# A two-layer hybrid trunk: layer 0's FFN and layer 1 run in context and latent halves, RWKV and GDN with one joint inverse and joint links

## The chip, the cores and the metric

The kernel runs on one core of a Trainium2 chip. TensorE (PE) does the matmuls into PSUM, VectorE (DVE), ScalarE (ACT) and GpSimd (POOL) the element work, SyncE (SP) issues the transfers between DRAM and SBUF. The metric is the device time of one execution in microseconds; of several runs the median is given.

## The reference

The input is 256 latent tokens `x` and 256 context tokens `ctx`, each of 1024 channels. Two layers follow one another. In each, four mixers read the same normed input, their outputs are gated and summed, and a SwiGLU FFN follows. The recurrent mixers start on the context, in both directions, and the latent half starts from the context's final state. `with_ctx` is true in layer 0 alone: layer 1 gives no context output, and of its context half only states, keys and values are used.

```python
def _rwkv7_mixer(pa, ca, ..., with_ctx):
    lat, ctx = _rwkv7_inputs(pa, ...), _rwkv7_inputs(ca, ...)
    for d in range(2):
        s_c, yc = _rwkv7_scan(ctx, d, s0, d == 1)
        _, yl = _rwkv7_scan(lat, d, s_c, d == 1)
    ...
def _mixer_block(h, hc, w_in, ...):
    p, pc = h @ w_in, hc @ w_in
    ...                     # RWKV-7, gated DeltaNet (GDN), GLA, window attention
    out = _merge((ya, yb, yg, yd), gl, gate_b, w_branch, w_out)
def _merge(ys, gate_pre, gate_b, w_branch, w_out):
    for i, y in enumerate(ys):
        g = sigmoid(gate_pre[..., i * D_MODEL:(i + 1) * D_MODEL] + gate_b[i])
        acc = acc + g * (y @ w_branch[i])
    return acc @ w_out
def _swiglu(h, w1, w2):
    gt, up = jnp.split(h @ w1, 2, axis=-1)
    return (jax.nn.silu(gt) * up) @ w2
```

## The kernel before

Channels lie on the partitions, tokens on the free axis, 512 columns: tiles 0 and 1 are the context, 2 and 3 the latents. A float32 product is made of three rounded ones. A weight block of 128x1024 (512 KB) is fetched as `raw`, rounded by ScalarE to `whi` (line 180), and VectorE subtracts to get `wlo` (line 183); with the input split into `hh` and `hl` a block gives 24 matmuls (16 with `whi`, 8 with `wlo`, line 193). Products go to three PSUM banks for this work: two of kind "f", one of kind "m".

`layer` (line 1383) does a whole layer. It norms the input, and makes the columns of `w_in` it needs: `dense_f` on all 512 columns for keys, values and states, in layer 1 on the 256 latent ones for queries and gates. `rwkv` and `gdn` bring the chunks of 64 tokens to triangular systems, and each inverts all of its own in `tri_inverse` (60 small VectorE operations on tiles `lx` and `lt`, a trip through DRAM tiles `dl`, `dx`, then products `v`). Then each has a chain of eight links, both directions in lockstep, whose small products (`psc`, 64x64) wait for one another through VectorE. High priority puts the inverse's steps and the links first. The 32 gate blocks (`w_gate`) have a low priority and fill what the chains leave; in GDN's chain `early` fills with the first 16 units of the merge (a unit is six matmuls with `yp`, a product with the gate `g`, and an addition into `acc1`). The other units and the last branch follow, then `residual` with `w_out`, and the FFN: 44 blocks of `ffn_w1`, whose hidden tiles are split at once into `uh` and `ul`, and 22 blocks of `ffn_w2` in `residual`. Beside layer 0's FFN `ada_f` (line 1245) makes layer 1's conditioning on VectorE: 160 products `gr` (or `gj`) of 128x512, line 1258.

The order of the instructions on each engine is set when the program is built, by a scheduler that takes them in the program's order and priority, with its own costs, as PSUM and SBUF buffers come free.

## Time and profile before

| | us |
|---|---|
| median of 3 runs | 1799.29 |
| lowest, highest run | 1786.75, 1800.61 |
| profiled execution | 1792.01 |
| its span | 1790.2 |
| TensorE busy | 1662.3 |
| VectorE busy | 1100.1 |
| ScalarE busy | 830.2 |
| GpSimd busy | 144.3 |
| mean granted TensorE clock | 0.958 |

Busy shares are means over stretches that differ. Layer 0's mixer ends at about 625 us, its merge and `w_out` at 717.5, its FFN at 1094; layer 1's mixer with merge and `w_out` ends at 1594.8, then comes its FFN. The clock is the share of full speed that was granted to TensorE.

### The profile page before, as it was taken

How to read it: one execution, taken by the hardware profiler on the slowest of the kernel's cores; microseconds unless marked ns; L12 is line 12 of the kernel's file. 1: busy time of each engine (PE TensorE's matmuls, PEld its weight loads, DVE VectorE, ACT ScalarE, POOL GpSimd, SP SyncE). 2: the span in 40 equal slices, each digit the busy share in tenths (PEclk: the TensorE clock that was granted, in tenths of full speed). 3: DMA queues.
4: the chain of work that ended last, by engine and by line, in shares of the span. 5: the costliest groups of instructions: out<-in, count | busy, mean ns of one | idle time of the engine just before them, and what ended most of it. 6: DMA issues, size and time to landing. Idle time of an engine off the chain costs nothing. (4 is left out here: it accounts for less than half of the span.)

```text
span 1790.2 us, 31565 instructions
## 1 busy us (share of the span) xinstructions
PE 1662.3 (93%) x12480; PEld 1328.0 (74%) x12480; DVE 1100.1 (61%) x2243; ACT 830.2 (46%) x1440; POOL 144.3 (8%) x255
## 2 busy tenths in 40 slices
PE   6999999998998979999999999998899869889998
PEld 3777775666786657888877888777777757779986
DVE  3466643447936765899675226666677665766654
ACT  3565442355534224544333226763556441366653
POOL 0000111000002250000000000002021002400000
PEclk8999999998999989999999999999999877989999
DMA  8322554442552363566775223334533461445553
GB/s 336 115 98 89 157 149 165 154 146 71 146 148 71 100 197 106 174 223 216 238 249 160 94 95 106 113 121 137 160 113 98 113 191 61 133 158 185 188 200 118
DMA packets 149684, 263.71 MB, mean 147 GB/s; under 512 B 62224, under 2 KB 77088, under 8 KB 149408
## 3 DMA queue, kind: packets, MB, share of 16 engines
q1 hardware_dynamic: 149536, 261.69, 45.9%
q8 instruction: 98, 1.61, 0.4%
q14 instruction: 50, 0.41, 0.1%
HBM read 236.12 MB, written 25.53 MB: 146 GB/s over the span
## 5 line engine op out<-in xcount | busy, mean ns | idle before, releaser
L193 PE MATMUL pd<-hh,whi 128*128 128x512 f32 (+1 forms) x1648 | 549.0, 352 | 17.9 <-ACT g L171 5.0
L193 PE MATMUL pd<-hl,whi 128*128 128x512 f32 (+1 forms) x1648 | 546.1, 349 | 0.2 <-DVE hl L183 0.2
L183 DVE TENSOR_TENSOR wlo<-raw,whi 128x1024 fp32r<-128x1024 f32 x280 | 347.1, 1242 | 266.4 <-ACT whi L180 112.9
L180 ACT ACTIVATE whi<-raw 128x1024 fp32r<-128x1024 f32 x280 | 295.9, 1057 | 423.9 <-PE pd L193 245.4
L193 PEld LDWEIGHTS pd<-hh,whi 128*128 128x128 f32 x1648 | 317.3, 193 | 72.0 <-issue 9.6
L193 PEld LDWEIGHTS pd<-hl,whi 128*128 128x128 f32 x1648 | 316.6, 193 | 44.3 <-issue 6.1
L193 PE MATMUL pd<-hh,wlo 128*128 128x512 f32 (+1 forms) x1648 | 340.0, 346 | 5.2 <-DVE wlo L183 5.2
L193 PEld LDWEIGHTS pd<-hh,wlo 128*128 128x128 f32 x1648 | 264.3, 190 | 47.5 <-DVE wlo L183 5.6
L193 PE MATMUL t<-whi,ul 128*128 128x512 f32 x264 | 104.4, 395 | 0.0
L193 PE MATMUL t<-whi,uh 128*128 128x512 f32 x264 | 104.3, 395 | 0.0
L1258 DVE SCALAR_TENSOR_TENSOR gr<-gr,crow 128x512 f32<-128x512 f32 x112 | 75.5, 688 | 27.5 <-DMA gr<-in_ada_t_dram 26.6
L193 PE MATMUL t<-wlo,uh 128*128 128x512 f32 x264 | 75.2, 395 | 0.0
L193 PE MATMUL pd<-yp,whi 128*128 128x512 f32 (+1 forms) x192 | 57.9, 410 | 15.9 <-DVE g L183 13.0
L171 ACT ACTIVATE g<-g 128x512 f32<-128x512 f32 (+1 forms) x128 | 66.5, 522 | 2.9
L183 DVE TENSOR_TENSOR th<-th,pd 128x512 f32<-128x512 f32 (+1 forms) x88 | 48.6, 552 | 26.6 <-PE pd L193 24.6
L183 POOL TENSOR_TENSOR acc<-acc,g 128x512 f32<-128x512 f32 (+1 forms) x48 | 56.4, 1191 | 72.2 <-DVE g L183 72.0
L180 ACT ACTIVATE uh<-th 128x512 fp32r<-128x512 f32 (+1 forms) x44 | 23.1, 526 | 78.5 <-DVE th L183 78.2
L193 PEld LDWEIGHTS t<-whi,uh 128*128 128x128 f32 x264 | 49.8, 188 | 11.5 <-DVE yr L183 0.2
L193 PEld LDWEIGHTS t<-wlo,uh 128*128 128x128 f32 x264 | 49.7, 188 | 11.5
L193 PEld LDWEIGHTS t<-whi,ul 128*128 128x128 f32 x264 | 49.8, 188 | 11.4
L171 ACT ACTIVATE g<-pd,P 128x512 f32<-128x512 f32 (+1 forms) x64 | 37.0, 577 | 45.2 <-PE pd L193 33.0
L193 PEld LDWEIGHTS pd<-yp,whi 128*128 128x128 f32 x192 | 34.5, 217 | 27.0 <-DVE g L183 16.1
(366 smaller groups left out, 2272.7 us busy)
## 6 DMA issues: line engine op xcount, KB each, us to landing
raw<-in_ffn_w_dram SPq DMA_DIRECT2D x132, 512.0 KB, 3.3
raw<-in_w_gate_dram SPq DMA_DIRECT2D x64, 512.0 KB, 3.5
gr<-in_ada_t_dram SPq DMA_DIRECT2D x112, 256.0 KB, 3.3
raw<-in_w_in_dram SPq DMA_DIRECT2D x52, 512.0 KB, 3.2
raw<-in_ada_w_dram SPq DMA_DIRECT2D x40, 512.0 KB, 5.7
gd<-g SPq DMA_DIRECT2D x32, 256.0 KB, 2.5
raw<-in_w_branch_dram SPq DMA_DIRECT2D x16, 512.0 KB, 3.6
g<-gd SPq DMA_DIRECT2D x32, 256.0 KB, 3.5
```

Of the source, the lines that this page charges most:

```text
L171: return self.nc.scalar.activation(out=out, in_=in_, func=func, bias=bias, scale=scale, **kw)
L180: return self.nc.scalar.activation(out=out, in_=in_, func=ACTF.Copy, scale=scale)
L183: return (eng or self.nc.vector).tensor_tensor(out=out, in0=a, in1=b, op=op)
L193: self.last = self.nc.tensor.matmul(out, lhsT=lhsT, rhs=rhs, start=start, stop=stop, skip_group_check=skip)
L1258: nc.vector.scalar_tensor_tensor(out=raw if v == nv - 1 else junk, in0=raw, scalar=1.0, in1=self.cr[:, v, 512 * h:512 * h + 512], op0=ALU. ...
```

## The change

From layer 0's FFN on, context and latents are separate. `layer0` still runs the mixer on 512 columns. Its FFN runs on the context (tiles 0, 1) first: `ffn_in` with 44 blocks at 256 columns, then `residual` with `ffn_w2`. Then `context1` does layer 1's context half: norm, 13 blocks of `w_in` and the two of `lv` at 256 columns, the systems of RWKV and GDN (four chunks each, into one tile `TT`), one `tri_inverse` for both, and four links in which RWKV and GDN with both directions, four generators, go in lockstep. Final states, keys and values stay in `keep`. The FFN of the latents comes behind `context1` in the program, with both products in the two "f" banks. `layer1` then works on 256 columns: it has again one inverse and four joint links, the gates as low-priority fill, then RWKV's output, and behind it all 24 units of `early` and the last branch. So 44 + 22 + 15 weight blocks are loaded, rounded and subtracted once more. The hidden tiles are stored in float32 and split per `w2` block. The products of `ada_f` get their pool before `w_out` of layer 0, and 96 of 160 must be done before `context1`. In layer 0 GLA's loads are moved ahead of GDN's inverse (`step(4)`).

```diff
...
+    def splits(self, hid):
+
+        def at(pool):
+            def parts(k, m):
+                h, l = [pool.tile([128, m, hid.shape[2]], F32R, tag=t, name=self.nm(t), bufs=4) for t in ("hh", "hl")]
+                self.split(h, l, hid[:, k:k + m])
+                return h, l
+            return parts
+        return at
...
+    def ffn_in(self, l, hh, hl, hid, t, fu, step):
+
+        w1 = self.A["ffn_w1"][l]
+        n = hh.shape[2]
+        for j in range(22):
+            pg = self.dense_f(w1[0, j], hh, hl, "f")
+            th = t.tile([128, n], F32, tag="th", name=self.nm("th"))
+            self.sig(th, pg[:, 0:n])
+            self.tt(th, th, pg[:, 0:n])
+            pu = self.dense_f(w1[1, j], hh, hl, fu[j % len(fu)])
+            self.tt(hid[:, j], th, pu[:, 0:n])
+            step(j)
...
+            step(4)
+            for _ in inv:
+                step(2)
+            e2.close()
+            step(4)
...
+        ta = self.pool("ada", 2, es=ea, side="right")
+        xt = {**self.xload(0, xl, (2, 3)), **self.xload(0, xc, (0, 1))}
...
-                pg = first.pop(0) if first else self.dense_f(w1[0, j], hh, hl, qts, "f")
-                th = t.tile([128, 512], F32, tag="th", name=self.nm("th"))
-                self.sig(th[:, 0:n], pg[:, 0:n])
-                self.tt(th[:, 0:n], th[:, 0:n], pg[:, 0:n])
-                pu = first.pop(0) if first else self.dense_f(w1[1, j], hh, hl, qts, "m" if nxt else "mf"[j % 2])
-                self.tt(th[:, 0:n], th[:, 0:n], pu[:, 0:n])
-                self.split(uh[:, j], ul[:, j], th[:, 0:n])
-                for _ in range(2):
-                    next(more, None)
-        self.mark("ffn2%d" % l)
...
+        self.norm_h(nx, A2, B2, [((0, 1), hhc, hlc), ((2, 3), hhl, hll)])
+        self.cr = self.crow(ta)
+        ada = chain(self.ada_f(0, 5, 1, mod2[:, 24:32], self.adab, ta, 2), prep(1, ta))
+        self.ffn_in(0, hhc, hlc, hid, t, "mf", lambda j: next(ada))
+        e1.close()
+        self.mark("ffn20")
+        nx = self.residual(A["ffn_w2"][0], self.splits(hid), (0, 1), mod2[:, 24:32], R_NG3, xt, True, e2, lambda: 1 in self.par or next(ada))
+        ctx.close()
+        while 1 not in self.par:
+            next(ada)
+        hid = self.pool("hidl", 1, es=lat).tile([128, 22, 256], F32, name=self.nm("hid"))
+        self.use(1)
+        self.context1(nx, xc)
+        self.use(0)
+        self.mark("ffn1l0")
+        self.ffn_in(0, hhl, hll, hid, t, "f", lambda j: next(ada, None))
+        self.mark("ffn2l0")
+        nx = self.residual(A["ffn_w2"][0], self.splits(hid), (2, 3), mod2[:, 24:32], R_NG3, xt, True, e2, lambda: next(ada, None),
+                           lambda: self.psf("f"))
+        run(ada)
+        self.xsave = self.dram.tile([2, 128, 1024], F32, name=self.nm("xsave"))
+        for t in (2, 3):
...
+            ds = self.dense_set(1, hh, hl)
+            main = self.pool("mc", 1, es=es, side="right")
+            self.cp(K.misc[64:128, 0:256], ds.col("misc")[64:128, 0:256])
+            rw = self.rwkv_tiles(main, 4, False)
+            gd = self.gdn_tiles(main, 4, False)
+            TT = main.tile([128, 2, 2, 8, 64], F32, name=self.nm("TT"))
+            rw.TT, gd.TT = TT[:, :, :, 0:4], TT[:, :, :, 4:8]
+            rw.keep, gd.keep = K.Z, K.S
+            st = self.tri_begin()
+            self.mark("rwkv1c")
+            self.rwkv_prep(1, rw, ds.col, st, 0, K.FB)
+            self.mark("gdn1c")
+            self.gdn_prep(gd, ds.col, K.misc[96:128, 0:256], st, 4)
+            vf = main.tile([128, 256], F32, name=self.nm("vf"))
+            more = chain(ds.attn_kv(K.ak[:, 0:256], K.av[:, 0:2], vf), ds.gla_kv(K.lk, K.lv[:, 0:2]))
+            self.mark("tri1c")
+            with ExitStack() as e2:
+                for _ in self.tri_inverse(st, TT, self.pool("tri", 1, es=e2)):
+                    next(more, None)
+            run(more)
+            self.mark("chain1c")
+            ch = self.pool("ch", 2, es=es, side="right")
+            for s in range(4):
+                with HP():
+                    lockstep([f(o, s, d, ch, i + d) for d in range(2) for i, (f, o) in ((0, (self.rwkv_link, rw)), (2, (self.gdn_link, gd)))])
+        self.mark("end1c")
+
...
+        st = self.tri_begin()
+        self.mark("rwkv1")
+        self.rwkv_prep(1, rw, ds.col, st, 0, K.FB)
+        self.mark("gdn1")
+        self.gdn_prep(gd, ds.col, K.misc[96:128, 256:512], st, 4)
+        with self.tc.high_priority(offset=-2000):
...
+        self.rwkv_resume(rw, K.Z, ch)
+        gd.S = [K.S[:, 0], K.S[:, 1]]
+        sr, sd = set(), set()
+        for s in range(4):
+            with HP():
+                got = lockstep([f(o, s, d, ch, i + d) for d in range(2) for i, (f, o) in ((0, (self.rwkv_link, rw)), (2, (self.gdn_link, gd)))])
+            for d in range(2):
+                self.rwkv_emit(rw, d, got[2 * d], Yr, sr)
+                gl(3)
+                self.gdn_emit(gd, d, got[2 * d + 1], Yg, sd)
+                gl(3)
+        self.mark("out1")
+        with HP():
+            self.rwkv_out(1, rw, Yr, K.misc[0:64, 256:512], ydst(0))
+            for b in range(2):
+                self.rms_gate(Yg[:, b].rearrange("p n e -> p (n e)"), ydst(1)(b), sg[:, b], P[:, R_GDNG:R_GDNG + 1],
+                              TT[:, 0, b, 0:4].rearrange("p n i -> p (n i)"))
...
+        gl(500)
+        gl(1000)
+        mx.close()
+        mg = self.pool("m1", 2, es=ac)
+        acc1 = self.pool("ac1", 1, es=ac).tile([128, KD, n], F32, name=self.nm("acc1"))
+        run(self.early(1, [(i, lambda i=i: yparts[i]) for i in (3, 0, 1)], gdr, acc1, mg))
...
```

The first place is VectorE at the end of GDN's chain of layer 0. `U` belongs to the chain, `yp`, `acc` and `g` to the merge, `kf`, `qf`, `AS` to GLA. Before:

```order
L183 TENSOR_TENSOR acc_826_4978<-g_5096,pd_5098 128x512
L183 TENSOR_TENSOR kf_4940<-lqk_4542,EP_5039 128x512
L190 SCALAR_TENSOR_TENSOR qf_4939<-lqk_4542,EN_5040 128x512
L183 TENSOR_TENSOR acc_826_4978<-g_5135,pd_5137 128x512
L183 TENSOR_TENSOR AS_4943<-m_5064,c_lmask_4933 128x512
L183 TENSOR_TENSOR acc_826_4978<-g_5224,pd_5226 128x512
L183 TENSOR_TENSOR U_5335<-psc,TK_3881 128x128
L183 TENSOR_TENSOR AS_4943<-m_5071,c_lmask_4933 128x512
```

After (the last link, then what follows it):

```order
L185 TENSOR_TENSOR U_5994<-psc,gd_3862 128x128
L185 TENSOR_TENSOR Y_5050<-Y_5050,Y_5996 128x2x64
L185 TENSOR_TENSOR Y_5050<-Y_5050,Y_6017 128x2x64
L185 TENSOR_TENSOR wlo_5937<-raw_5934,whi_5936 128x1024
L185 TENSOR_TENSOR TT_3864<-Y_5050,TT_3864 128x512 x2
L192 SCALAR_TENSOR_TENSOR Y_5050<-TT_3864,P_105,sg_3773 128x512 x2
L185 TENSOR_TENSOR yp_5113<-y_5114,yp_5112 128x512
L185 TENSOR_TENSOR yp_5113<-y_5118,yp_5112 128x512
L185 TENSOR_TENSOR yp_5041<-Y_5050,yp_5040 128x512 x2
L185 TENSOR_TENSOR yp_5043<-lqk_4542,yp_5042 128x512
L185 TENSOR_TENSOR acc_842_5036<-g_5128,pd_5130 128x512
L185 TENSOR_TENSOR yp_5043<-lqk_4542,yp_5042 128x512
```

The products into `acc` of the first branch stood among the links (`U`, `Y`) and stand now behind the last of them.

The second place is VectorE where the inverse begins; `lx` and `lt` are its tiles, `th` and `hid` the latent FFN's. GDN's inverse in layer 1 before:

```order
L183 TENSOR_TENSOR lt_13370<-lt_13370,lx_13369 128x19x12
L183 TENSOR_TENSOR lx_13369<-lt_13370 128x234
L183 TENSOR_TENSOR lt_13370<-lt_13370,lx_13369 128x18x13
L183 TENSOR_TENSOR lx_13369<-lt_13370 128x238
L183 TENSOR_TENSOR lt_13370<-lt_13370,lx_13369 128x17x14
L183 TENSOR_TENSOR wlo_13702<-raw_13699,whi_13701 128x1024
L183 TENSOR_TENSOR lx_13369<-lt_13370 128x240
L183 TENSOR_TENSOR lt_13370<-lt_13370,lx_13369 128x16x15
```

The joint inverse of the context after, at its start:

```order
L185 TENSOR_TENSOR hid_9061<-th_11484,pd_11495 128x256
L185 TENSOR_TENSOR wlo_11566<-raw_11563,whi_11565 128x1024
L324 COPY lt_10083<-lx_10082 64x1024
L185 TENSOR_TENSOR th_11558<-th_11558,pd_11533 128x256
L185 TENSOR_TENSOR hid_9061<-th_11558,pd_11569 128x256
L185 TENSOR_TENSOR lx_10082<-lt_10083 128x30
L185 TENSOR_TENSOR lt_10083<-lt_10083,lx_10082 128x30
L185 TENSOR_TENSOR lx_10082<-lt_10083 128x58
L185 TENSOR_TENSOR lt_10083<-lt_10083,lx_10082 128x29x2
```

The last rows of the latent FFN (`th`, `hid`) before the steps stand there; the same inverse after, at its 28th step (128x17x14):

```order
L185 TENSOR_TENSOR lx_10082<-lt_10083 128x234
L185 TENSOR_TENSOR lt_10083<-lt_10083,lx_10082 128x18x13
L185 TENSOR_TENSOR lx_10082<-lt_10083 128x238
L185 TENSOR_TENSOR lt_10083<-lt_10083,lx_10082 128x17x14
L185 TENSOR_TENSOR wlo_10267<-raw_10264,whi_10266 128x1024
L185 TENSOR_TENSOR lx_10082<-lt_10083 128x240
L185 TENSOR_TENSOR wlo_11604<-raw_11601,whi_11603 128x1024
L185 TENSOR_TENSOR lt_10083<-lt_10083,lx_10082 128x16x15
L185 TENSOR_TENSOR lx_10082<-lt_10083 128x240
```

In both the steps stand in one piece up to 128x17x14; after, the pieces of the latent FFN (`hid`, `th`, the next `wlo`) stand ahead of and behind that piece.

The third place is TensorE in a chain. GDN's chain of layer 1 before (`psc` the links, `pd` merge units, `Y` the outputs):

```order
L193 MATMUL Y_14860<-qi_13211,S_14754 64x64 x3
L193 MATMUL psc<-S_14754,ke_13210 64x64 x4
L193 MATMUL psc<-S_14757,ke_13210 64x64 x4
L193 MATMUL Y_14860<-qi_13211,S_14754 64x64
L193 MATMUL pd_14872<-yp_14497,wlo_14781 128x256
L193 MATMUL Y_14881<-qi_13211,S_14757 64x64 x4
L193 MATMUL pd_14893<-yp_14497,whi_14780 128x256
L193 MATMUL pd_14893<-yp_14498,whi_14780 128x256
L193 MATMUL pd_14893<-yp_14497,whi_14780 128x256
```

The joint chain of the context after (`pd` a block of the latent FFN, `psc` the links):

```order
L195 MATMUL psc<-rw_9153,TT_9161 64x64 x3
L195 MATMUL psc<-gd_9155,TT_9161 64x64 x4
L195 MATMUL pd_11980<-hh_6675,whi_11976 128x256
L195 MATMUL pd_11980<-hh_6676,whi_11976 128x256
L195 MATMUL pd_11980<-hh_6675,whi_11976 128x256
L195 MATMUL pd_11980<-hh_6676,whi_11976 128x256
L195 MATMUL psc<-rw_9153,TT_9161 64x64
L195 MATMUL pd_11980<-hh_6675,whi_11976 128x256
L195 MATMUL pd_11980<-hh_6676,whi_11976 128x256
L195 MATMUL pd_11980<-hh_6675,whi_11976 128x256
L195 MATMUL pd_11980<-hh_6676,whi_11976 128x256
L195 MATMUL pd_11980<-hh_6675,wlo_11977 128x256 x4
```

The products of two branches now stand next to each other, and the cover between them is one FFN block in place of merge units.

## Rows read from the trace of the kernel before

**Rows 1.** The page, busy time of each engine (us, share of the span, instructions).

```profile
PE 1662.3 (93%) x12480; PEld 1328.0 (74%) x12480; DVE 1100.1 (61%) x2243; ACT 830.2 (46%) x1440; POOL 144.3 (8%) x255
```

**Rows 2.** Stretches: length, busy time of engines (x instructions), granted clock, DMA share, GB/s.

```profile
625.00:717.50 92.50, 77.72 (x311) 58.59 (x309) 55.05 (x72) 35.83 (x73) 27.76 (x19) 0.94 0.48 149
717.50:1094.00 376.50, 374.97 (x1680) 305.18 (x1681) 242.28 (x524) 142.75 (x214) 0.00 (x0) 0.99 0.53 175
1094.00:1594.80 500.80, 438.88 (x4399) 367.86 (x4397) 341.53 (x732) 260.00 (x503) 65.08 (x121) 0.91 0.43 129
1594.80:1790.20 195.40, 188.25 (x1321) 176.04 (x1321) 109.65 (x147) 105.88 (x168) 0.00 (x0) 0.98 0.50 167
```

**Rows 3.** Layer 1's mixer in eight stretches, columns as in group 2.

```profile
1094.00:1110.00 16.00, 13.38 (x86) 11.57 (x85) 14.17 (x26) 15.15 (x35) 0.24 (x3) 0.89 0.58 198
1110.00:1228.00 118.00, 109.42 (x992) 95.69 (x991) 77.38 (x121) 80.83 (x142) 6.96 (x15) 1.00 0.41 123
1228.00:1288.00 60.00, 51.44 (x457) 43.36 (x457) 39.31 (x93) 25.04 (x50) 4.91 (x7) 0.93 0.51 142
1288.00:1362.00 74.00, 71.27 (x849) 54.51 (x847) 54.44 (x127) 38.66 (x79) 16.60 (x48) 0.94 0.28 93
1362.00:1419.00 57.00, 50.36 (x539) 44.31 (x540) 39.84 (x71) 37.42 (x76) 5.85 (x7) 0.91 0.41 116
1419.00:1472.00 53.00, 37.94 (x360) 33.62 (x358) 36.65 (x86) 20.57 (x40) 0.16 (x1) 0.83 0.63 174
1472.00:1538.00 66.00, 60.23 (x891) 47.93 (x890) 40.13 (x142) 12.85 (x23) 13.43 (x22) 0.77 0.23 73
1538.00:1594.80 56.80, 44.84 (x238) 36.87 (x238) 39.61 (x72) 29.49 (x61) 16.93 (x18) 0.87 0.57 189
```

**Rows 4.** Matmuls of line 193 in two stretches of 50 us (512 columns, 256 columns).

```profile
1000.00:1050.00 50.00, 50.00 (x216) 40.44 (x215) 1.00 0.28 95
1600.00:1650.00 50.00, 50.00 (x424) 50.00 (x423) 1.00 0.55 180
```

**Rows 5.** A stretch of layer 0's FFN; layer 1's FFN: w1, w2.

```profile
750.00:850.00 100.00, 100.00 (x430) 80.44 (x429) 96.55 (x240) 40.81 (x54) 0.00 (x0) 1.00 0.66 218
...
1594.80:1722.40 127.60, 127.60 (x1061) 127.21 (x1062) 79.41 (x116) 82.06 (x137) 0.00 (x0) 0.99 0.53 177
1722.40:1783.00 60.60, 60.60 (x261) 48.83 (x260) 28.07 (x28) 22.64 (x28) 0.00 (x0) 1.00 0.44 150
```

**Rows 6.** Groups of instructions (busy, mean ns of one): page, then three stretches of VectorE.

```profile
L183 DVE TENSOR_TENSOR wlo<-raw,whi 128x1024 fp32r<-128x1024 f32 x280 | 347.1, 1242 | 266.4 <-ACT whi L180 112.9
L180 ACT ACTIVATE whi<-raw 128x1024 fp32r<-128x1024 f32 x280 | 295.9, 1057 | 423.9 <-PE pd L193 245.4
L1258 DVE SCALAR_TENSOR_TENSOR gr<-gr,crow 128x512 f32<-128x512 f32 x112 | 75.5, 688 | 27.5 <-DMA gr<-in_ada_t_dram 26.6
...
L1258 DVE DVE_READ_ACCUMULATOR gr<-gr,crow 128x1 f32 x112 | 9.1, 81 | 0.0
...
L183 DVE TENSOR_TENSOR ul<-th,uh 128x256 fp32r<-128x256 f32 x22 | 9.2, 418 | 0.0
...
L183 DVE TENSOR_TENSOR g<-g,pd 128x512 f32<-128x512 f32 x11 | 7.4, 684 | 11.7 <-DMA g<-gd 11.7
```

**Rows 7.** VectorE in time, GDN's inverse: first and 28th step (start, length, instruction).

```profile
1422.09 0.20 DVE L183 TENSOR_TENSOR lx<-lt 128x30 f32<-128x30 f32 x1 [1.01 <-DMA lt<-dl]
...
1431.84 0.41 DVE L183 TENSOR_TENSOR lt<-lt,lx 128x238 f32<-128x238 f32 x1
```

**Rows 8.** Waits of TensorE, 1094 to 1362 us (total, times, longest).

```profile
PE S L193 <- POOL aq L183: 5.6, 1, 5.6
PE v L193 <- DMA TT<-dx: 2.9, 1, 2.9
```

**Rows 9.** GpSimd in layer 1's mixer.

```profile
L183 POOL TENSOR_TENSOR acc<-acc,g 128x256 f32<-128x256 f32 x24 | 22.2, 943 | 27.2 <-DVE g L183 27.0 <-DVE gc L183 0.2
```

**Rows 10.** The page, bytes moved in 40 equal slices of the span.

```profile
GB/s 336 115 98 89 157 149 165 154 146 71 146 148 71 100 197 106 174 223 216 238 249 160 94 95 106 113 121 137 160 113 98 113 191 61 133 158 185 188 200 118
```

More of the change, by code (lines that the diff above doesn't have):

```diff
@@ new lines, in gdn_prep @@
+                tokens(QK[:, b, 0], o.kt[:, b])
+                more()
+            if o.out:
+                for b in range(2):
+                    norm(b, 1)
+                for b in range(2):
+                    pr = c3(psw())
+                    for n in range(N):
+                        tk = slice(64 * n, 64 * n + 64)
+                        for rw in rws:
+                            self.mm(pr[rw, n], QK[rw, b, 0, tk], QK[rw, b, 1, tk])
+                    for d in range(2):
+                        z = c3(qi[:, d, b])
+                        self.tt(z, z, c3(QK[:, b, 1]))
+                        self.tt(At[:, d, b], At[:, d, b], pr)
+                    more()
@@ L1339, in gtiles, with residual @@
         return G
-    def residual(self, w, hh, hl, tiles, mod, ng, xt, norm, eo, fill=None):
+    def residual(self, w, parts, tiles, mod, ng, xt, norm, eo, fill=None, bank=None):
         yp = self.pool("nrm", 1, es=eo, side="right")
@@ new lines, in merge @@
+    def merge(self, l, i, y, gd, acc, p, ah, al):
+        nc = self.nc
+        n = acc.shape[2]
+        for hf in range(2):
+            w = self.wload(self.A["w_branch"][l, i, hf], "mf"[hf])
+            for fb in range(4 * hf, 4 * hf + 4):
+                g = p.tile([128, n], F32, tag="g", name=self.nm("g"), bufs=3)
+                nc.sync.dma_start(out=g, in_=gd[fb, :, i])
+                pb = self.ps()
+                self.branch(pb, w, y, fb - 4 * hf)
+                self.tt(g, g, pb[:, 0:n])
+                self.tt(acc[:, fb], acc[:, fb], g, ALU.add, eng=nc.gpsimd)
+                self.split(ah[:, fb], al[:, fb], acc[:, fb])
@@ new lines, in layer0 @@
+        hp = self.pool("h1", 1, es=hs)
+        hh, hl = [hp.tile([128, KD, T], F32R, name=self.nm("hh")) for _ in range(2)]
+        self.norm_h(xs[2], Ac, Bc, [(tiles, hh, hl)])
+        xs[0].close()
+        ds = self.dense_set(0, hh, hl)
+        mp = self.pool("mx", 1, es=mx, side="right")
+        misc = mp.tile([128, T], F32, name=self.nm("misc"))
+        pm = ds.col("misc")
+        with ExitStack() as e:
+            self.shift_mix(pm, 7, misc, self.pool("ms", 1, es=e, side="right"), rows=64)
@@ L1641, in layer @@
-        self.mark("ffn2%d" % l)
-        if not full:
-            uh, ul = _Shift(uh), _Shift(ul)
-        nx = self.residual(A["ffn_w2"][l], uh, ul, tiles, mod2[:, 24:32], R_NG3, xt, bool(nxt), eo, lambda: next(more, None))
-        run(more)
-        hid.close()
-        lay.close()
-        if nxt:
-            self.xsave = self.dram.tile([2, 128, 1024], F32, name=self.nm("xsave"))
-            for t in (2, 3):
-                nc.sync.dma_start(out=self.xsave[t - 2], in_=xt[:, t])
-        return xo, xt, nx
+        self.mark("ffn10")
```

1435 lines of the change are left out of this document (715 added, 720 removed).

## The prediction

> **What bounds the kernel now.** I read the page's first section, then tables of stretches, then rates, then the waits. TensorE is busy for 93% of the span [rows 1], so the kernel is a stream of matmuls, and a change can win only where that stream stops or runs at the lower clock. The stretches show where that is. Between 717.5 and 1094 us (layer 0's FFN) PE is busy 375.0 of 376.5 us at a clock of 0.99; in the last 195 us (layer 1's FFN) it is the same. Layer 1's mixer is different: 438.9 busy of 500.8 us at a clock of 0.91 [rows 2]. Its eight segments [rows 3] give the loss place by place. Idle time is length minus PE busy; the clock's loss I take as length times (1 - clock). Norm and preparation (1094 to 1228): 11.2 idle and 1.8 clock, 13. RWKV's inverse and chain (1228 to 1362): 8.6+4.2 and 2.7+4.4, 20. GDN's preparation: 6.6+5.1, 12. GDN's inverse: 15.1+9.0, 24. GDN's chain: 5.8+15.2, 21. Merge and w_out: 12.0+7.4, 19. Together 109, which leaves 392 us of matmuls at full clock. So the second half of this mixer, where the cover of the first half is used up, loses 57 us; that is the prize.
>
> **FFN in halves.** A 512-column matmul starts every 50/216 = 0.231 us, a 256-column one every 50/424 = 0.118 us, both at a clock of 1.00 [rows 4]. Two halves cost 0.236, 2% more. A whole FFN half is in the trace: layer 1's takes 127.6 us for w1 and 60.6 for w2 [rows 5]. Twice that is 376.4 us against the 376.5 of layer 0's FFN now. For TensorE the split is free, although 66 weight blocks are read, rounded and subtracted twice: the 24 x 0.118 = 2.8 us of a block cover ScalarE's 1.06 and VectorE's 1.24 us for it [rows 6].
>
> A rule speaks against halves. The Trainium skill (TensorE: Matmul & The Clock Gate, section "Why this matters for your kernels") wants every dimension of a matmul at 512 or more, and its "Back-to-back issue gap" gives 81 ns sustained at 128 columns and 131 at 512; 98 in between would be my estimate from that page for 256, so a pair would cost 196 against 131, and the FFN alone would grow by over 100 us. The rates above contradict it by measurement, and I give that case no chance of its own.
>
> VectorE has to be asked too. The adaLN products (L1258, 160 in all, 0.69 us each [rows 6]) ran beside layer 0's whole FFN. In one stretch of that FFN VectorE was 97% busy and PE still 100% [rows 5], so a high load alone does no harm. After the change about 60 products lie in layer 0's merge and w_out, some 60 in the context's w1 half and 28 in its w2 half. The w1 half: 79.4 us [rows 5] less 22 splits of 0.42 (9.2), plus 64 x 0.77 with the accumulator read, 119 of 127.6 [rows 6]: hidden. The w2 half: 28.1 [rows 5] plus 22 splits of a pair of hidden tiles at about 0.69 (15.2, as 128x512 elements cost in g<-g,pd) plus 28 x 0.77 (21.5) is 65 against PE's 60.6. It becomes VectorE's: **+6 us** with the end of its queue. If everything overlapped it would be 0, if ScalarE and VectorE alternated 12.
>
> **Layer 1 twice, in halves.** 13 w_in blocks and the two of lv run for both halves: 15 x 24 x 2 matmuls of 0.118 against 15 x 24 of 0.231, **+2 us**. The small products are the same ones (each chunk, each direction), so the 392 us of work stay, only in two places: about 85 us (42 of them the 15 blocks) beside the latent FFN, about 310 on the latent half. What changes is what is lost around it, in the segments' terms:
> - latent norm and preparation: 13 now. VectorE's work halves with the columns, but GDN's preparation joins it: 16.
> - context preparation: it lies beside FFN matmuls, but all FFN products of the latent half use the two "f" banks. As GDN's preparation now, 11.
> - two joint inverses. RWKV's, with the gates beside it, lost 13; GDN's, with little cover, 24. A joint one has the same number of steps (60 operations, the first 28 of them in 1422.1 to 1432.2 us, about 10 us [rows 7], over both branches at once, as its lanes hold 8 chunks). At their high priority the 28 stand in one piece ahead of the next wlo; in the order of the changed context inverse only one product (pd_11569) and its predecessor are ready then, 2 x 24 x 0.118 = 5.7 us, so some 5 us of the 10 are open, with the fetch of the inverse over DRAM (2.9 us wait [rows 8]) and the clock behind. 13 each: 26.
> - two joint chains of four links. The two chains of now take 74 and 66 us for eight links each, 8 to 9 a link; four branches and directions in lockstep fill each other's gaps, and each chain has FFN or gate products between its links, as the first of the two has now (7): 14.
> - the output of RWKV, now in front of the merges: 3.
> - merge and w_out: 19 now. 16 of the 24 early merge units leave the chain and stand behind it, where POOL's addition (0.94 us each [rows 9]) runs beside 6 x 0.118 = 0.71 of matmuls; 24 x 0.23 is 6 more: 25.
>
> Sum 95 against 109: **-14 us**. For the bounds: the inverses 7 each at the least (the first one's 13, less attention's wait of 5.6 us in it [rows 8]), 24 at the most; the chains 2 (idle of the first) to 21 each; the rest a third either way.
>
> **Layer 0.** The step that puts GLA's loads ahead moves gate products into GDN's chain, and eight units of the branch-0 merge out of it, behind its last link (the rows in the order). 8 x 6 x 0.231 = **+11 us** between the chain's end and the FFN. That stretch is 92.5 us with VectorE busy 55 [rows 2]; with 8 units (0.68 each) and 60 adaLN products (46 us) added VectorE has 106 of 104: it bounds here too. 0 if the gates moved in were the ones that PE waited for, 20 if the adaLN products stand ahead of the residual.
>
> **Sum.** The profiled execution took 1792.0 us (1790.2 of span). +6 +2 -14 +11 = +5: 1797. Before's runs have a median 7 us above that execution, so the same place among runs is **1804**. That is the forecast: no difference (a measurement here can tell about 1%, 18 us; before's own three runs spread over 14).
>
> **Rivals.**
> *Faster, the interleaving works as the stretches allow.* The latent FFN is 188 us of matmuls that need nothing from layer 1, and context work beside it would lose nothing; one joint inverse and one joint chain on the latent half with all 32 gates (32 x 24 x 0.118 = 91 us) as cover would lose what the first pair lost (13 and 7), preparation 13, merge 19. Loss 52 instead of 95: -43, so 1761. If layer 0 then costs nothing, 1750. For it: the 57 us of GDN's part were lost with the gates used up. Against: the order puts 18 of the gates into the latent preparation and 6 behind the chain, and two "f" banks carry the context part. The Trainium skill (Perfetto Trace Analysis, section "Optimization Strategy") says that regimes with different limits can gain by being interleaved, which is this case; here the trace agrees in that FFN stretches run at clock 0.99 and the mixer at 0.91.
> *Slower, the high-priority VectorE work starves the two-bank fill.* In the context part VectorE has 70 us for the latent w1 half and, by its share of the mixer's 341.5 [rows 2], about 100 more, against 127.6+85 of PE: 0.80 on average, but its inverse, scan and chain rows come in blocks ahead of the silu and product that free a bank. If the stretch loses an inverse as GDN's does now (24), a chain as GDN's (21), and a preparation of 18, the context costs 63 instead of 31: +32, so 1836. It decides once a free "f" bank comes later than the 2.8 us that one block's matmuls last, for most of the stretch. The same section of the skill reads repeating gaps on the busiest engine as a sign of too few PSUM or SBUF buffers; no such gap stands in the FFN stretches of before, which had three banks.
> *Slower, the weights.* 81 blocks more of 0.5 MB each are fetched, 42 MB. In the context's w2 half 11.5 MB of weights and 7 MB of adaLN rows in 61 us are 300 GB/s; before's mean in any 45-us slice reached 336 once, 249 next [rows 10]. At 250 that half takes 74 us: +13, so 1817; it would need no other loss to be slower.
>
> **Chances.** Forecast (within 18 us) 0.38; faster 0.32; slower by starvation 0.22, by weights or layer 0's VectorE bunching 0.08. So faster by over 1%: 0.32, within 1%: 0.38, slower: 0.30. The likeliest's own range is 1786 to 1820. Eight in ten reach from the faster case (1761, with its unknowns to 1752) to the starved one (1836, with the inverses at their most 1842).
>
> **What would show it.** Right: PE's busy share between the context's norm and the last matmul of the latent w2 about 0.9 with a clock of 0.95, and that context stretch (188 + 85 + 31) near 304 us; the context's w2 half at 65 us with VectorE above 0.95; layer 1's latent mixer at about 370 us with the joint inverse idle for 8 or more, and 100 us between layer 0's chain and FFN. Wrong towards faster: the context stretch near 275 us, the latent mixer under 345. Wrong towards slower: the waits of pd for th or wlo dominate in the context stretch, and it passes 325; or raw weights land late in it. If the time moves by over 18 us and the stretch from 717 us on does not, layer 0's reordering was the mis-sized step.

## The result

The changed kernel takes 1894.59 us (median of 4 runs, 1890.12 to 1903.9) against 1793.67 (1786.75 to 1800.61) of the kernel before: 1.0569 times as long, 95% interval [1.0502, 1.0636]. About the same was forecast, 1804 with 1752 to 1842; it is slower by 101 us, further than any rival had put it. The profiled execution has a span of 1888.2 us at a clock of 0.950.

The page, busy time of each engine, which answers [rows 1], and the bytes moved in 40 slices, which answers [rows 10]:

```profile
PE 1695.1 (90%) x13745; PEld 1405.8 (74%) x13745; DVE 1232.9 (65%) x2508; ACT 949.2 (50%) x1731; POOL 147.0 (8%) x275
...
GB/s 319 111 101 105 152 167 144 162 114 86 147 64 136 216 192 144 252 292 285 303 164 121 110 163 169 135 190 148 157 155 137 119 114 118 142 154 191 189 190 123
```

TensorE is busy 33 us longer, the span is 98 us longer: two thirds of the loss is TensorE standing still. The stretches tell where. First the kernel before, cut at the end of layer 0's GDN chain, at the last transpose ahead of each FFN and of layer 1's mixer (the columns are those of [rows 2]):

```profile
617.10:725.00 107.90, 92.67 (x423) 71.11 (x423) 66.69 (x94) 43.81 (x90) 31.61 (x22) 0.92 0.47 148
725.00:1103.80 378.80, 374.76 (x1679) 304.09 (x1678) 245.02 (x528) 146.43 (x223) 0.14 (x2) 1.00 0.54 178
1103.80:1592.00 488.20, 428.82 (x4352) 359.57 (x4350) 331.44 (x713) 248.47 (x474) 64.94 (x119) 0.91 0.42 127
```

The changed kernel: layer 0's merge and w_out, the FFN's context half, the context half of layer 1 with the latent FFN, layer 1's latent mixer, its FFN:

```profile
588.30:746.40 158.10, 118.94 (x458) 86.41 (x458) 126.29 (x235) 52.10 (x104) 39.39 (x26) 0.89 0.63 197
746.40:963.00 216.60, 201.98 (x1379) 186.63 (x1379) 183.86 (x386) 117.96 (x192) 0.10 (x1) 0.97 0.80 264
963.00:1287.80 324.80, 288.91 (x2600) 261.47 (x2599) 213.65 (x416) 177.17 (x337) 13.58 (x43) 0.93 0.50 152
1287.80:1689.30 401.50, 340.86 (x3332) 296.95 (x3331) 260.54 (x580) 216.14 (x456) 49.09 (x95) 0.93 0.45 139
1689.30:1888.20 198.90, 189.96 (x1333) 176.93 (x1333) 116.77 (x149) 110.51 (x172) 0.00 (x0) 0.98 0.51 165
```

Layer 0's chain ends 28.8 us earlier, without the merge units in it, but the stretch behind it grows by 50.2: the FFN starts 21.4 us later. From there to layer 1's FFN it is 942.9 us against 867.0, 75.9 more. The end is as before. Taking as loss the idle time (length less busy) plus length times (1 - clock), in pieces of 20 us, the 867 us held 758 of work and 109 of loss; the 943 hold 771 and 172. So the halves add 13 us of work and 63 of loss, where the forecast for all of it was -6.

### The profile page after: what moved, and what is told of

It reads as the page before. It is cut to its first block, busy times and chain, and to the rows that moved or that the text cites. A ratio compares the mean times of both kernels' runs of the same rounds, so it can differ in the third digit from the quotient of the medians.

```text
span 1888.2 us, 35035 instructions
## 1 busy us (share of the span) xinstructions
PE 1695.1 (90%) x13745; PEld 1405.8 (74%) x13745; DVE 1232.9 (65%) x2508; ACT 949.2 (50%) x1731; POOL 147.0 (8%) x275
## 5 line engine op out<-in xcount | busy, mean ns | idle before, releaser
L195 PE MATMUL pd<-hh,whi 128*128 128x256 f32 (+1 forms) x4112 | 694.0, 317 | 22.7 <-DVE th L185 10.7
L195 PEld LDWEIGHTS pd<-hh,whi 128*128 128x128 f32 x4112 | 581.2, 194 | 89.5 <-DVE th L185 12.7
L182 ACT ACTIVATE whi<-raw 128x1024 fp32r<-128x1024 f32 x361 | 380.8, 1057 | 524.0 <-PE pd L195 307.6
L185 DVE TENSOR_TENSOR wlo<-raw,whi 128x1024 fp32r<-128x1024 f32 x361 | 444.5, 1234 | 225.8 <-ACT whi L182 156.8
L195 PE MATMUL pd<-hh,wlo 128*128 128x256 f32 (+1 forms) x2056 | 357.8, 313 | 10.7 <-DVE wlo L185 10.7
L195 PE MATMUL t<-whi,hh 128*128 128x512 f32 (+1 forms) x348 | 103.7, 356 | 0.0
L195 PE MATMUL t<-whi,hl 128*128 128x512 f32 x220 | 86.9, 397 | 2.1 <-DVE hl L185 2.1
L195 PE MATMUL t<-wlo,hh 128*128 128x512 f32 (+1 forms) x284 | 75.6, 376 | 11.9 <-DVE wlo L185 11.7
L195 PEld LDWEIGHTS t<-wlo,hh 128*128 128x128 f32 x284 | 50.2, 193 | 23.1 <-DVE wlo L185 13.8
L195 PEld LDWEIGHTS t<-whi,hh 128*128 128x128 f32 x348 | 57.4, 190 | 10.5 <-ACT UV L182 0.8
L195 PE MATMUL t<-whi,ah 128*128 128x512 f32 x192 | 55.9, 406 | 2.6 <-DVE g L185 2.6
```

The lines of the kernel that those rows point to most:

```text
L182: return self.nc.scalar.activation(out=out, in_=in_, func=ACTF.Copy, scale=scale)
L185: return (eng or self.nc.vector).tensor_tensor(out=out, in0=a, in1=b, op=op)
L195: self.last = self.nc.tensor.matmul(out, lhsT=lhsT, rhs=rhs, start=start, stop=stop, skip_group_check=skip)
```

## The experiments

All times are medians of four runs where nothing else is said; kernels that ran together shared their runs of the kernel before, and the ratio is to those. The stretches are cut as above; they are those of one profiled execution of each kernel, so they need not add up to the difference of the medians. The edits are shown shortened.

**1. The adaLN rows, fetched once.** In `ada_f`:

```diff
-                    raw = pool.tile([128, 512], F32, tag="gr", ...)
-                    nc.sync.dma_start(out=raw, in_=self.A["ada_t"][...])
+                    raw = self.gr0        # fetched at the first call alone
```

> The changed kernel with the rows of the adaLN matrix fetched once and used for all 160 products, so that 40 MB of transfers are gone and every product on VectorE stays (layer 1's conditioning is then wrong). Transfers bound the context half of layer 0's FFN (742 to 966 us, DMA share 0.78 to 0.87, raw blocks late): that stretch goes from 224 to about 200 us, layer 0's merge stretch (594 to 742) loses about 5, the kernel takes about 1865 us. VectorE bounds it (85% busy there): both stay within 5 us, 1890 to 1900.

1879.96 us (1.0455 [1.0404, 1.0506]), 15 us less than the changed kernel. (The products write to a tile of their own here, of two buffers, in place of their input of three.)

**2. The adaLN products on 32 columns.**

```diff
-      scalar_tensor_tensor(out=raw ..., in0=raw, in1=self.cr[:, v, 512 * h:512 * h + 512],
+      scalar_tensor_tensor(out=raw[:, 0:32] ..., in0=raw[:, 0:32], in1=self.cr[:, v, 512 * h:512 * h + 32],
```

> The changed kernel with the 160 adaLN products on 32 columns in place of 512, the transfers of their rows kept (the conditioning is then wrong): about 0.5 us of VectorE less per product. Transfers bound the context half: 742 to 966 us stays within 8 us of 224, the kernel 1880 to 1895. VectorE bounds it: the stretch falls to about 200, the merge stretch by 15 to 20, the kernel takes about 1855.

1877.89 us (1.0440 [1.0377, 1.0504]), 17 us less. The context half of the FFN, first without the transfers, then without the products:

```profile
750.20:951.80 201.60, 196.91 (x1387) 183.88 (x1386) 176.06 (x366) 119.35 (x194) 0.10 (x1) 0.99 0.56 180
```

```profile
740.90:948.80 207.90, 199.56 (x1378) 185.02 (x1376) 135.07 (x307) 118.71 (x195) 0.09 (x1) 0.98 0.76 254
```

216.6 us became 201.6 and 207.9. Neither theory holds alone: transfers are the larger part (15 us), VectorE the smaller (9), and without the products the merge stretch is 5 us shorter. In the changed kernel ScalarE waits for raw weight blocks in that half; its waits from 746.4 to 890 us (total, times, longest):

```profile
ACT whi L182 <- DMA raw<-in_ffn_w_dram: 40.4, 13, 5.3
ACT whi L182 <- PE pd L195: 19.5, 14, 4.3
```

Behind whi stand wlo and the block's matmuls, and with 264 GB/s in this half a block of ffn_w lands in 4.6 us (median) where layer 1's FFN before got it in 3.3.

**3. GLA's loads of layer 0 back to where they were.**

```diff
             self.mark("gtri0")
-            step(4)
+            step(0)
```

> The changed kernel with one number put back: GLA's loads in layer 0 come after the inverse's first step again, not four steps ahead of GDN's inverse. The order then has the first merge units among the links of GDN's chain again. If their move behind the chain is what layer 0 lost (chain end to FFN 148 us, before 92.5, chain end 30 us earlier): FFN starts 20 us earlier, the kernel takes about 1873. If the adaLN products and transfers in the merge are what it lost: FFN starts within 6 us of 742, the kernel 1888 to 1900.

1877.10 us (1.0450 [1.0393, 1.0506]), 17 us less; the FFN starts at 725.0, as in the kernel before. So with two gate tiles it is the order of layer 0 that costs the 21 us; adaLN's products, which stay in this kernel's merge, are at most the 5 us of run 2. Why the place costs so much, the next run tells.

**4. More buffers for the merge's gate tiles.**

```diff
-            self.arp = self.pool("m1", 2, es=ac)
+            self.arp = self.pool("m1", 4, es=ac)      # layer 0
-        mg = self.pool("m1", 2, es=ac)
+        mg = self.pool("m1", 6, es=ac)                # layer 1
```

> The changed kernel with the gate tiles of the early merge units in 4 buffers (layer 0) and 6 (layer 1) in place of 2, nothing else. If the merge units wait for the fetch of their gate tile (VectorE waits for g from DRAM, SyncE for GpSimd to free one): layer 1's merge (1597 to 1657 us) falls from 60 to about 42, layer 0's stretch by 10 to 15, the kernel takes about 1865. If GpSimd's addition or VectorE paces them: layer 1's merge stays at 55 to 60, the kernel at 1888 to 1900.

1844.13 us (1.0258 [1.0207, 1.0309]): 50 us less, half of what the change lost, by two numbers. Layer 1's merge falls from 60 to 42 us (1569.6 to 1611.8 here), as the first theory had it. Waits behind layer 0's chain in the changed kernel, first VectorE, SyncE's queue and TensorE from 588.3 to 690 us:

```profile
DVE acc L185 <- DMA g<-gd: 9.2, 6, 2.7
...
SPq L1413 <- POOL acc L185: 28.8, 14, 3.6
...
PE pd L195 <- DVE g L185: 14.8, 9, 3.0
...
PE pd L195 <- DVE acc L185: 5.7, 4, 3.7
```

then TensorE in x4, 586.4 to 690 us:

```profile
PE pd L195 <- ACT yp L182: 5.2, 2, 2.6
PE m L195 <- DVE g L185: 4.7, 3, 2.6
PE pd L195 <- DVE g L185: 2.9, 2, 1.4
```

TensorE's waits for `g` and `acc` fall from 23 to 8.5 us. VectorE's own waits for a gate tile do not (14.7 us in x4, 11.5 in the changed kernel).

A unit's gate tile comes from DRAM in 4.6 us (median), and with two tiles the fetch of unit n+2 can be issued only when unit n has freed its tile. So a unit takes half of that round and not its 1.38 us of matmuls. In the first branch VectorE's product into `acc` frees the tile. Three such units in the changed kernel, TensorE in order of time (start, length): they start 2.2 to 2.5 us apart.

```profile
604.99 1.20 PE L195 MATMUL pd<-yp,whi 128*128 128x512 f32 x4 [0.54 <-DVE acc L185]
...
607.53 1.19 PE L195 MATMUL pd<-yp,whi 128*128 128x512 f32 x4 [0.87 <-DVE acc L185]
...
609.72 1.19 PE L195 MATMUL pd<-yp,whi 128*128 128x512 f32 x4 [0.55 <-DVE acc L185]
```

In the later branches GpSimd's addition frees it. Each fetch is issued as an addition ends, and the units start 2.8 to 3.7 us apart (644 to 663 us):

```profile
646.99 1.67 POOL L185 TENSOR_TENSOR acc<-acc,g 128x512 f32<-128x512 f32 x1 [1.24 <-DVE g L185]
648.68 0.33 SPq L1413 DMA_DIRECT2D g<-gd  x1
...
649.89 1.67 POOL L185 TENSOR_TENSOR acc<-acc,g 128x512 f32<-128x512 f32 x1 [1.23 <-DVE g L185]
651.59 0.33 SPq L1413 DMA_DIRECT2D g<-gd  x1
```

The stretches of x4:

```profile
586.40:717.80 131.40, 111.57 (x468) 85.53 (x468) 99.48 (x189) 53.23 (x106) 35.80 (x26) 0.92 0.68 214
717.80:940.20 222.40, 204.34 (x1387) 188.74 (x1386) 194.10 (x417) 118.93 (x192) 0.00 (x0) 0.96 0.81 266
940.20:1256.90 316.70, 284.21 (x2576) 257.38 (x2574) 216.50 (x430) 175.10 (x333) 12.50 (x44) 0.94 0.50 157
1256.90:1647.60 390.70, 340.94 (x3345) 297.31 (x3346) 262.24 (x581) 217.86 (x459) 53.02 (x95) 0.93 0.47 144
```

Layer 0's stretch is 26.7 us shorter, layer 1's latent half 10.8. The context stretch is 8.1 shorter and the context's FFN half 5.8 longer; no merge lies in either, so these two are not the gate tiles' doing but go with a new order.

**5. The context inverse at the program's priority**, on top of 4.

```diff
-            for _ in self.tri_inverse(st, TT, ...):
+            for _ in self.tri_inverse(st, TT, ..., off=1):   # priority offset, was 20000
```

> The kernel of x4_more_gate_tiles (1844 us), with the steps of the context's joint inverse at the program's own priority in place of the high one. If the steps in one piece starve the latent FFN's two banks (TensorE waits for wlo 5.8, 6.6 and for whi there): the stretch from the context's norm to layer 1's norm (317 us) falls to about 305, the kernel to 1832. If the inverse's own length is what the stretch waits for at the end: it grows by up to 15, 1845 to 1860.

1845.66 us (1.0302 [1.0251, 1.0353]): no difference to 1844; the context stretch is 321.8 us. But the edit did not move the steps. At the program's own priority VectorE still runs the first 27 in one piece, and TensorE's wait for the `wlo` behind them is the same. VectorE's first step, its next `wlo`, and TensorE; first x4, then this run:

```profile
1085.35 0.20 DVE L185 TENSOR_TENSOR lx<-lt 128x30 f32<-128x30 f32 x1
...
1094.96 1.22 DVE L185 TENSOR_TENSOR wlo<-raw,whi 128x1024 fp32r<-128x1024 f32 x1
...
1096.23 2.08 PE L195 MATMUL t<-wlo,hh 128*128 128x256 f32 x8 [6.57 <-DVE wlo L185]
```

```profile
1085.65 0.20 DVE L185 TENSOR_TENSOR lx<-lt 128x30 f32<-128x30 f32 x1
...
1095.28 1.22 DVE L185 TENSOR_TENSOR wlo<-raw,whi 128x1024 fp32r<-128x1024 f32 x1
...
1096.55 2.08 PE L195 MATMUL t<-wlo,hh 128*128 128x256 f32 x8 [6.81 <-DVE wlo L185]
```

So this run says nothing on the rival of the prediction, that the steps in one piece starve the fill; run 13 does.

**6. The latent links apart**, on top of 4 (with three gate tiles in layer 1, for room).

```diff
-            got = lockstep([f(o, s, d, ch, i + d) for d in range(2) for i, (f, o) in (rwkv, gdn)])
+            got = lockstep([self.rwkv_link(rw, s, d, ch, d) for d in range(2)])
+        # RWKV's output, then for s in range(4):
+            got = lockstep([self.gdn_link(gd, s, d, ch, 2 + d) for d in range(2)])
+            # and four merge units after each
```

> The kernel of x4_more_gate_tiles, but in the latent half of layer 1 RWKV's four links run first, then its output, then GDN's four links with 16 merge units as cover (3 gate tiles there instead of 6, for room); the inverse stays joint. If the joint links cost by leaving every merge unit behind the chain: the latent half (391 us) falls to about 375, the kernel to 1828. If the joint links gain what they are for: the chain grows by 25 or more and the half is 395 to 410, the kernel 1848 to 1863.

1851.82 us (1.0330 [1.0280, 1.0379]), 8 us more, but the latent half itself is 391.9 us against 390.7 (4 of the 8 arose in layer 0, where nothing was edited). Neither theory's number came for the half. The chain itself grew from 71 us (1473.3 to 1544.7) to 115 (1473.7 to 1588.9), so the joint links do gain time; the merge, part of it now beside the links, gave as much back. Three gate tiles in place of six count against this run.

**7. Runs 3 and 4 together.**

> The kernel of x4_more_gate_tiles with GLA's loads in layer 0 back behind the inverse's first step (x3). x3 alone gave 17 us, x4 50. If the units behind the chain cost because each waited for its gate tile: with four tiles the place of the units no longer matters, layer 0's FFN starts at 715 to 722 as in x4, 1840 to 1848. If the place costs by itself: FFN starts near 705, 1828.

1843.16 us (1.0281 [1.0224, 1.0339]): as run 4 alone, and the FFN starts at 719.7 against 717.8. So the 17 us of run 3 and the 50 of run 4 are not two gains: where the units stand does not matter once their tiles come in time.

**8. The kernel before with more gate tiles.**

```diff
-            self.arp = self.pool("m1", 2, es=ac)
+            self.arp = self.pool("m1", 3 if full else 6, es=ac)
```

> The kernel before with the merge units' gate tiles in 3 buffers (layer 0; there is room for no more) and 6 (layer 1) in place of 2. If the fetch of the gate tiles was a cost there already (VectorE waits 13.5 us for g behind layer 0's chain): 1778 to 1786. If its chain covers the fetch: 1790 to 1800, and the gate tiles are a cost that the change brought.

1776.97 us (9 runs, 0.9911 [0.9884, 0.9937]): 17 us less than the kernel before, and the fastest of all. So the fetch was a cost there as well, of 17 us, and about three times that in the changed kernel (50), in which no merge unit of layer 0's first branch and almost none of layer 1's first three has a chain beside it. With more tiles in both (layer 0 has 3 here and 4 in run 4), the change still costs 67 us.

**9. Neither adaLN's transfers nor its products**, on top of 4 (edits 1 and 2 together).

> The kernel of x4_more_gate_tiles (1844 us) with the adaLN rows fetched once and the 160 products on 32 columns (the conditioning is then wrong): neither transfers nor VectorE work of adaLN beside the context half. x1 and x2 took 15 and 9 us off that half one at a time. If the two are what holds it: 718 to 940 us (222) falls to 195 to 200, the kernel to about 1815. If the halves of 256 columns have a floor of their own (fetch of raw blocks with two buffers): 208 or more, the kernel 1828 or more.

1830.74 us (1.0213 [1.0185, 1.0242]). The context half is 199.1 us, as the first theory had it, though not the whole:

```profile
715.40:914.50 199.10, 193.95 (x1379) 181.50 (x1377) 124.33 (x163) 120.22 (x195) 0.00 (x0) 1.00 0.57 185
914.50:1239.80 325.30, 287.91 (x2595) 259.28 (x2595) 213.70 (x415) 176.57 (x336) 13.57 (x43) 0.93 0.49 150
```

The context half is 23 us shorter, the context stretch 8.6 longer, the latent half 5 shorter. The profiled executions differ by 21 us, the medians by 13. With the order set anew at each build, a gain in one stretch does not carry over whole.

**10. The latent FFN on all three banks**, on top of 4.

```diff
-        self.ffn_in(0, hhl, hll, hid, t, "f", ...)
+        self.ffn_in(0, hhl, hll, hid, t, "mf", ...)
```

> The kernel of x4_more_gate_tiles with the latent FFN's second product alternating between the m and f buffers (weights, raw blocks and PSUM banks), as the context half and layer 1's FFN do, in place of f alone. If the two f banks starve the context stretch: 940 to 1257 us (317) falls by 15 or more, the kernel to 1828. If the context's own blocks need the m buffers as much: unchanged or up to 10 longer, 1840 to 1855.

1878.02 us (1.0465 [1.0432, 1.0498]), 34 us more; the context stretch is 350.0 us. That is the second theory's sign at three times its size: the one m bank, with its single whi and wlo, is better left to the context's blocks.

**11. w_in alternating between m and f as well.**

```diff
-        o.col = lambda name: self.dense_f(A["w_in"][l, WCOL[name]], hh, hl)
+        # f = "mf"[q % 2], q counts the calls
+        o.col = lambda name: self.dense_f(A["w_in"][l, WCOL[name]], hh, hl, f)
```

> As x10, and layer 1's w_in blocks alternate between the m and f buffers as well (m has one whi and one wlo, f two). If the single whi and wlo of m slows the preparations (context 124 us, latent 118): each loses 5 to 10 less, the kernel 1825 to 1835. If the preparations wait for their own chains of small products: 1840 to 1855.

1935.76 us (1.0794 [1.0744, 1.0844]). The context stretch is 343.0 us, 7 less than in run 10, but the latent half goes from 390.7 to 464.1. Its preparation gains as the first theory had it (111 us to the inverse's first load, against 124); from that load to the inverse's last product it takes 202 us against 93, and what holds it there stays open. Of the three ways tried, the fill on two banks of its own was the best.

**12. A third buffer for fetched f blocks**, on top of 4, through the FFN's halves and the context stretch.

> The kernel of x4_more_gate_tiles with a third buffer for fetched weight blocks of kind f through layer 0's FFN halves and the context stretch (there is no room for more). A block's matmuls take 2.8 us at 256 columns; its fetch lands 3.8 to 4.3 us after issue and its buffer is held 2.3 more, so two buffers give one block each 3.1 to 3.3 us. If that cadence bounds the halves: 718 to 940 falls to about 205, the context stretch by 10, the kernel to 1820. If transfers bound the first by their rate and VectorE the second: within 6 us of 1844.

1832.45 us (1.0210 [1.0183, 1.0236]), 12 us less. The context half:

```profile
722.80:930.20 207.40, 197.84 (x1367) 184.64 (x1365) 192.17 (x408) 120.04 (x193) 0.14 (x2) 0.97 0.84 276
```

222.4 became 207.4 at a higher rate of transfer (276 GB/s), so the rate itself was not at its end: what bound was one fetch per 256-column block with two buffers. ScalarE's waits for a raw block in the first 137 us of that half, 31.3 us in x4, are gone. The context stretch gave only 3.6.

**13 and 14. The inverses' steps left out**, in x4's kernel and in x8's (layer 1).

```diff
-        for k in range(1, 31):
+        for k in (() if self.short else range(1, 31)):
```

> The kernel of x4_more_gate_tiles (1844 us) without the 60 VectorE steps of layer 1's two joint inverses (the transfers and products of the inverse stay; the result is then wrong). If the steps and the wait for them are what the inverse stretches lose (20 us in the context's 75, 31 in the latent's 85): the context stretch and the latent half fall by 15 to 25 each, the kernel to 1800. If the loss lies in the transfers, in attention and in the used-up gates: 0 to 10 each, the kernel 1825 to 1844.

> The kernel of x8_before_more_tiles (1777 us) without the 60 steps in each of layer 1's two inverses (result then wrong), to compare with x13. If an inverse costs the same in both kernels: as much off 1777 as x13 takes off 1844, so the halves' 67 us lie elsewhere. If the gates cover RWKV's inverse here: 10 to 25 in all, 1752 to 1767, and less than x13's.

1834.00 (1.0221 [1.0176, 1.0267]) and 1794.44 us (10 runs, 1.0001 [0.9978, 1.0025]). The first is 10 us less (18 in the profiled execution: 5 in the context stretch and 15 in the latent half, 375.3 us). In the context stretch TensorE's wait behind the steps (6.6 us in x4) is gone, but TensorE then waits for the inverse's own trip through DRAM instead:

```profile
PE v L195 <- DMA ta<-dm: 8.8, 1, 8.8
...
PE v L195 <- DMA TT<-dx: 4.7, 1, 4.7
```

The second is 17 us more than x8, with less to do: layer 1's mixer went from 479.6 to 491.7 us, and it starts 7 us later, although nothing ahead of it was edited. Without the steps the two kernels lie 40 us apart in place of 67. But that is not the price of the steps, as most of it is the second kernel's growth: the scheduler lays out another order, and that moves the time by as much as the steps. What can be said is that the steps hold 10 us of the changed kernel (20 by the two stretches), and not 67.

**15. The latent FFN held back until the context's blocks are through**, on top of 4.

```diff
-        hid = self.pool("hidl", 1, es=lat).tile([128, 22, 256], F32, ...)
         self.use(1)
         self.context1(nx, xc)
         self.use(0)
+        hid = self.pool("hidl", 1, es=lat).tile([128, 22, 256], F32, ...)
```

> The kernel of x4_more_gate_tiles with the latent FFN's hidden tile allocated after context1, where it takes the room of the context's h: the latent FFN can then start only when the context's blocks are through, so that it covers the inverse and the chain, but not the preparation. If the cover of the preparation is worth what the change is for: the context stretch (317 us) grows by 30 or more, the kernel to 1875 or above. If preparation and FFN get in each other's way (VectorE, weight buffers): within 12 us of 1844.

1907.68 us (1.0631 [1.0569, 1.0694]), 64 us more, nearly all of it in the context stretch (316.7 in x4):

```profile
944.90:1323.10 378.20, 301.44 (x2576) 272.32 (x2574) 221.83 (x431) 177.01 (x333) 11.72 (x44) 0.85 0.43 132
```

So the cover works: without the latent FFN beside its preparation the context stretch is 61 us longer. That is a comparison within the split kernel, and not with the kernel before.

## Why the prediction was wrong, step by step

- **Layer 0, +11, measured +21** (588.3 to 746.4 us against 617.1 to 725.0). The order was read right, eight units behind the chain. The price was wrong: the units were costed at their matmuls, 1.38 us, when [rows 2] had the hint, 92.5 us of merge and w_out with PE busy only 77.7. Runs 4, 7 and 8 show that a unit behind the chain takes the round of its gate tile with two buffers. VectorE, said to bound that stretch, was busy 126 of 158 us.
- **Merge of layer 1, 19 to 25.** The same mistake: 24 units were costed by GpSimd's 0.94 us [rows 9]. From 1597 to 1657 us TensorE was busy 38.8 of 60 us; with six tiles the merge takes 42 us and the latent half is 10.8 shorter. GpSimd paced through the tile that it frees, not by its own speed.
- **FFN halves, +6, measured about +19** (against 127.6 and 60.6), 13 of them in the part that was called hidden. In the changed kernel's context half the w1 part and the w2 part are

```profile
746.40:887.00 140.60, 130.27 (x1051) 128.56 (x1050) 119.40 (x266) 74.08 (x120) 0.00 (x0) 0.97 0.80 263
887.00:953.80 66.80, 63.67 (x267) 50.54 (x267) 56.48 (x108) 35.57 (x51) 0.10 (x1) 0.97 0.80 267
```

  The step that failed is "119 of 127.6: hidden". VectorE's 119 came out to the microsecond, but the w1 part took 140.6 us: VectorE alone was weighed there, and not the transfers. With the adaLN rows fetched once (run 1) it takes 126.4 us, and the ACT waits of run 1 and the third buffer of run 12 show how: by late raw blocks. The w2 part took 66.8 against 65, though not by VectorE, which was busy 0.85 of it and not above 0.95. The weights rival named the right cause for the wrong part: it had w2 at 74 us. The other 9 us up to 963 are the context's norm, with TensorE busy 8.0 us, mostly on the latent FFN. That two halves cost TensorE no more than the whole was right: run 9, without adaLN, takes 127.2 and 62.1 us.
- **Layer 1 in halves: work +2, measured +13 with the FFN's; loss -14, measured +48.** The table has the loss by part. An inverse is cut from the first load of its tiles to its last product, the links from there to the last product into `psc`; "before" is the whole mixer, RWKV's and GDN's parts where there are two. The forecast has the latents' norm in the 16 of their preparation. Figures are rounded.

| part | forecast | changed kernel | x4 | before |
|---|---|---|---|---|
| context's preparation | 11 | 22 | 21 | |
| its inverse | 13 | 21 | 18 | 14 (RWKV) |
| its links | 7 | 1 | 4 | 6 (RWKV) |
| from there to the end of the latents' norm | | 16 | 10 | |
| latents' preparation | 16 | 10 | 11 | 9 + 12 |
| their inverse | 13 | 33 | 33 | 26 (GDN) |
| their links | 7 | 2 | 2 | 19 (GDN) |
| outputs, merge, w_out | 28 | 46 | 30 | 18 |
| sum | 95 | 151 | 129 | 103 |

  The joint links did what they were for: 3 us of loss where 14 were forecast and the two chains before had 25. What was mis-sized, besides the merge, are the joint inverses, 26 against 55 (the latent one beyond its bound of 24), and the context's preparation. The context stretch took 325 us in place of 304, the latent mixer 401 in place of 370. In the context's inverse "some 5 us of the 10 are open" was nearly all of the 10: while VectorE runs the 28 steps (1107.07 to 1117.1 us) TensorE is busy 1.6 us, and it waits for the `wlo` behind them.

```profile
1107.00:1117.00 10.00, 1.58 (x14) 1.37 (x12) 9.01 (x29) 1.01 (x2) 0.00 (x0) 0.79 0.01 3
```

```profile
1117.13 1.22 DVE L185 TENSOR_TENSOR wlo<-raw,whi 128x1024 fp32r<-128x1024 f32 x1
...
1118.41 1.86 PE L195 MATMUL t<-wlo,hh 128*128 128x256 f32 x7 [9.82 <-DVE wlo L185]
```

- **The rivals.** The faster one fell: the stretches did not lose less. The starvation rival came nearest in the context stretch, 63 of loss named and 60 measured, but partly by luck: its links lost 1 us and not 21, and 16 lie behind them, up to the end of the latents' norm, which it did not have. Its mechanism is real at one place, the steps ahead of `wlo` above, at 10 us of 325; no run took the priority away, as run 5 left the order as it was, and without the steps (run 13) 5 us of that stretch were won. A third bank for the fill, taken from the context's blocks, made it worse (run 10); a bank more for both was not tried. The weights rival was right in its cause, in the w1 part, and too small. No rival had the gate tiles, the largest single cause.
- **Range.** It was made from mechanisms that were added one at a time. The gate tiles in both layers and the raw blocks of the FFN half, each a transfer through two buffers whose cover was gone or halved, came on top of the inverses.

**What the 101 us are made of**, so far as runs show it: 50 are gate tiles, of which the kernel before paid 17 itself, so 34 by the change. The other 67 lie between x4 and x8, 70 in their profiled executions: the context's FFN half is 34 us longer than half of x8's FFN (222.4 against 188.5), the context stretch and the latent half together 39 longer than the other half and x8's mixer (707.4 against 668.1), and the two ends are 4 shorter. Of the 34, adaLN accounts for 23 (run 9) and the third fetch buffer for 15 (run 12); the two overlap, since both act in that half. In the medians they gave 13 and 12. The 39 are about 8 of work and 31 of loss, and these stay largely **open**: the table says where they lie, in the context's preparation, the inverses and the merge, but no run took them away, except for the inverses' steps (run 13). No single wait holds them. The largest in the changed kernel's context stretch (963 to 1287.8 us) and latent half are

```profile
PE t L195 <- DVE wlo L185: 9.8, 1, 9.8
PE pd L195 <- DVE wlo L185: 6.5, 1, 6.5
PE h L198 <- DVE rs L185: 4.2, 1, 4.2
```

```profile
PE pd L195 <- DVE acc L185: 11.2, 5, 5.3
PE pd L195 <- DVE g L185: 9.0, 6, 2.5
PE PT L198 <- DVE P L189: 5.2, 3, 4.0
```

the first pair of the latter being the merge. The rest are many waits of a few us for a preparation, an inverse or a norm, which now occur twice; that they are a fixed cost of each half is argued from the list, not shown, and runs 13 and 14 could not separate it.

## What to carry to other kernels

Work that leaves the cover of a chain must be priced by its slowest round, the fetch and the release of its buffer, and not by its matmuls; count the buffers of everything that is moved. Where a split halves the matmuls of a weight block, the block's fetch stays whole, so the fetch's round over its buffers is to be held against the new, shorter time of a block. And before a large change it pays to look for a wait at a small pool in the kernel as it is: two numbers gave 0.991 [0.9884, 0.9937] here, more than the change could.

## What the runs showed that was not expected

A block of 512 KB lands in 3.3 us at 177 GB/s (layer 1's FFN in the kernel before) and in 4.6 at 264 (context half of the changed one), while a third buffer raised the rate there to 276, at 4.5 us: landing time grew before the rate stopped growing.

Changing a step's priority need not move it: run 5 took the inverse's priority away, and VectorE's order around its steps stayed as it was. An edit meant to test an order has to be checked in the trace before its time is read. And leaving 120 VectorE steps out made a kernel 17 us slower (x14 against x8): with an order laid out anew at each build, differences of 10 to 17 us between two builds are no evidence of a mechanism without the stretch in which they fall.
